# Source order for every engine beside the inverse, the scan and the output groups of a hybrid decoder layer, and two early x tiles

## Chip, cores and metric

The kernel runs on one core of one Trainium2 chip. The metric is the device time in microseconds of one execution, as the median of several runs. The profile is one further execution, taken by the hardware profiler.

## What is computed

One decoder layer on x of shape (1, 2048, 1024), float32:

```python
h = rms_norm(x, norm_w)
proj = h @ w_in                        # 1024 -> dn_qkv, dn_z, dn_b, dn_a, swa_q/k/v, swa_z, gates
o_dn = gated_delta_rule_chunked(...)   # 4 heads of 128, chunks of 64: a triangular solve per chunk,
                                       # then a scan over chunks with state S (128 x 128 per head)
o_dn = rms_norm(o_dn, dn_norm_w) * silu(dn_z)
for window, dilation in ((128, 1), (512, 4), (2048, 16)):
    ...                                # dilated sliding-window attention, o and its log denominator
o_swa = sum(softmax(lse over the three groups) * o) * silu(swa_z)
merged = sigmoid(g_dn) * (o_dn @ w_branch_dn) + sigmoid(g_swa) * (o_swa @ w_branch_swa)
out = x + merged @ w_out
```

## The kernel before

All large products are taken in two parts: each operand is split into a high part (ScalarE, `AF.Copy` into fp32r, L90) and the rest (VectorE or GpSimd, a subtraction, L91), and a product is three matmuls, high by high, high by low, low by high. The profile calls the engines PE (TensorE), ACT (ScalarE), DVE (VectorE), POOL (GpSimd) and SP (the queue from which the DMAs are issued).

TensorE's program is one long list. Everything else is hung on it by a clock of ticks: after every six of the large matmuls the kernel calls `hook()`, and `self.at(n, f)` calls f at the n-th hook from then. So the order of the source is a plan by hand: what stands at a tick is written into the program between the matmuls of that tick. Whether an engine's instructions run in that order is another question. Inside `tc.manual_schedule(engines=...)` the engines named keep the source's order; the others are ordered by a planner, by its own estimates of cost. `pinned(False)` names PE, ACT, DVE and POOL, `pinned(True)` SP as well. Each engine works its list off in order, each instruction waiting for what it needs.

The stages in the order of time:

- 0 to about 970 us: the projection for the attention (L436) with the attention beside it. Pinned; not touched.
- about 970 to 1990: `cunits`, 36 units of 128 columns of `w_in`. A unit has four blocks of 512 tokens, a block 24 matmuls of 512 columns (L723 to L725) into one of three "mm" PSUM tiles. Its weights come by DMA and are split in two halves, the next unit's at the fourth and the eighth hook after the first block of this one (`c_part`: ACT L90, POOL L91). Gate units (`g_block`) have ACT take tanh (L1161) out of PSUM into one of two "gt" tiles, which SP writes to DRAM (gscr, L1163); z units (`z_block`) do the same and add a VectorE operation (L1153) that reads PSUM once more.
- beside `cunits`, first the DeltaNet preparation (everything but SP pinned), and from `start_inverse` on, at about 1408 us, the following, with only PE pinned:
  - the inverse: VectorE reads Z (all 128 chunks' matrices, one per partition) and solves row by row, rows 1 to 63; a row is a product (L1023), two memsets and a sum (L1026), all on VectorE, and each row sets a tick for the next, more ticks the longer the row is. Row 64 copies (L1018) and writes the result to DRAM (vscr L1015, tscr L1019). The same ticks carry `combine(t)`, t = 0 to 15, ten ticks each, which merges the three attention groups: sums on VectorE (L1260, L1261), an exponential on ACT (L1262), shares and three weighings on VectorE (L1265 to L1271), two additions on POOL (L1276), and a write to osd by SP (L1278). `combine(0)` is called eight ticks after the inverse is set up.
  - the scan, at about 1768 to 1950: sixteen steps of three ticks, for two pairs of heads each. Stage 0: products with the state S into an "sc" tile (L1084, L1086), then rr on VectorE (L1088) and qs on ACT (L1091). Stage 1: a product (L1095), copied by ACT (L1097). Stage 2, for each pair: a product (L1101) into the single "po" tile, the state's update on VectorE (L1103), a product (L1106), its sum on VectorE (L1109), squares on ACT (L1113), a short chain on POOL (L1116 to L1120), and the scaling on VectorE (L1122), all of pair 0 and then all of pair 1 in the source. After both pairs `prep` for the next step: in stage 1 a product into an "sc" tile that VectorE reads (L1062, L1065), in stage 2 one that ACT reads (L1070, L1072). There are two "sc" tiles. The records of step t + 2 are loaded by SP at the end of step t.
  - from the last units on, the first weights of the next stage are loaded and split (`tail`, `w_split`).
- about 1990 to 2189: the fin phase, branch projections and gates, in eight blocks (`fin_y`), under `pinned(True)`. Products of weights for the output are formed beside it; two of them, T1 and T4, are parked in DRAM by way of the staging tiles "th" and "tl" of the pool `lp`, and fetched back in the last block.
- about 2189 to the end: eight output groups of 256 tokens (`group`), each seven Strassen-Winograd products of twelve matmuls (L1421 to L1423). The merged rows come back from DRAM as "mt" tiles (`m_load`, one group ahead), are summed and split four products ahead (`m_op`), the results are kept or added in "hold" tiles (ACT L1400, VectorE L1402, L1408), the residual x in "xo" tiles (loaded at the start of each group, four of 256 KB) is added, and SP writes the result. No engine is pinned here.

Of the kernel before, what the change touches and what calls it, by code (L numbers as in the profile page):

```python
# [6 lines left out]
F32 = mybir.dt.float32  # L7
F32R = mybir.dt.float32r
# [4 lines left out]
P = 128  # L13
T = 2048
D = 1024
# [28 lines left out]
def dr(ap, off, dims):  # L44
    return bass.AP(tensor=ap.tensor, offset=ap.offset + off, ap=[list(d) for d in dims])


class Net:
# [1316 lines left out]
    def m_op(self, q):  # L1365
# [8 lines left out]
        def new(n, a, b, how):  # L1374
            ss[n] = self.rawp.tile([P, 4, P], F32, name="raw")
            V.tensor_tensor(out=ss[n], in0=a, in1=b, op=how)  # L1376
# [8 lines left out]
        elif i == 4:  # L1385
            new("S4", part["A12"], ss["S2"], ALU.subtract)

    def group(self, g):
        nc, V, p2 = self.nc, self.nc.vector, self.p2
        acc, xo = {}, {}  # L1390
        hold = {"p1": p2.tile([P, 512], F32, name="hold", bufs=5)}

        def x_load(t, c):
            xo[t, c] = p2.tile([P, 512], F32, name="xo", bufs=4)
            nc.sync.dma_start(xo[t, c], dr(self.i["x"], (2 * g + t) * P * D + c * 512, [[D, P], [1, 512]]))

        def keep(n, pr, add=None):
            t = hold[n] = hold.get(n) or p2.tile([P, 512], F32, name="hold", bufs=5)
            if add is None:
                nc.scalar.activation(t, pr, AF.Copy)  # L1400
            else:
                V.tensor_tensor(out=t, in0=pr, in1=add, op=ALU.add)  # L1402

        def plus(n, t, c):
            nc.gpsimd.tensor_tensor(out=hold[n], in0=hold[n], in1=xo.pop((t, c)), op=ALU.add)

        def result(t, c, pr, add):
            V.tensor_tensor(out=add, in0=pr, in1=add, op=ALU.add)  # L1408
            nc.sync.dma_start(dr(self.out, (2 * g + t) * P * D + c * 512, [[D, P], [1, 512]]), add)
        for t, c in ((0, 0), (0, 1), (1, 1), (1, 0)):  # L1410
            x_load(t, c)
        if g == 0:
            self.m_load(1)
        for i, (_, tgt, first, wn) in enumerate(PROD):
            q = 7 * g + i
            self.at(1, lambda q=q: self.m_op(q + 4))
            if first:
                acc[tgt] = self.ps.tile([P, 512], F32, name="mm", bufs=3)
            pr = acc[tgt]
            ah, al = self.m_slot(q)  # L1420
            wh, wl = self.W[wn]  # L1421
            for k in range(4):
                mm = lambda x, y, **kw: nc.tensor.matmul(pr, x, y, **kw)  # L1423
                mm(ah[:, k, :], wh[:, k, :], start=first and k == 0, stop=False, skip_group_check=True)
                mm(ah[:, k, :], wl[:, k, :], start=False, stop=False, skip_group_check=True)
                mm(al[:, k, :], wh[:, k, :], start=False, stop=(k == 3), skip_group_check=True)
                if k % 2:
                    self.hook()
            if i == 0:
                keep("p1", pr)  # L1430
            elif i == 1:
                keep("u2", pr, hold["p1"])
                plus("u2", 0, 1)
            elif i == 2:
                result(0, 0, pr, xo.pop((0, 0)))
            elif i == 3:
                keep("u3", pr, hold["p1"])
                plus("u3", 1, 1)
                plus("p1", 1, 0)
            elif i == 4:  # L1440
                result(1, 1, pr, hold["u3"])
            elif i == 5:
                result(1, 0, pr, hold["p1"])
            else:
                result(0, 1, pr, hold["u2"])

    def run(self):
        from functools import partial
        tc = self.tc
# [3 lines left out]
        E = mybir.EngineType  # L1453
        pinned = lambda sync: tc.manual_schedule(engines={E.PE, E.Activation, E.DVE, E.Pool} | ({E.SP} if sync else set()))
# [53 lines left out]
        pin = ExitStack()  # L1508
# [9 lines left out]

        def start_inverse():
            self.nb_out()  # L1520
            pin.close()
            pin.enter_context(tc.manual_schedule(engines={E.PE}))
            dst.close()
            self.cb = pool(bst, "cb")
            self.inverse(pool(ist, "ip", "right"), start_scan)
# [31 lines left out]
        gu = [partial(self.g_block, j) for j in range(16)]  # L1557
        du = [partial(f, h) for h in range(H) for f in (self.k_block, self.q_block, self.v_block)]
        self.cunits(zu[:3] + du + gu[:12] + zu[3:] + gu[12:], {3: open_dn, 15: lambda: self.at(9, start_inverse)}, tail)
        self.flush()  # L1560
        pin.close()
# [7 lines left out]
        with pinned(True):  # L1569
            for nb in range(8):  # L1570
                if nb < 7:
                    self.o_plan(nb + 1, 4)
                if nb == 0:
                    for c in range(4):
                        self.at(1 + 28 * c, lambda c=c: self.wo_chunk(c))
                if nb == 7:
                    self.m_load(0)
                for m in range(8):
                    self.fin_y(nb, m)
                    if nb == 7 and m in (1, 3):  # L1580
                        self.fetch("T1" if m == 1 else "T4")
                    if nb == 7 and m < 4:
                        self.at(4, lambda m=m: self.m_op(m))
            self.flush()
        fst.close()
        self.p2 = pool(p2st, "p2", "right")
        for g in range(8):
            self.group(g)
        self.flush()
        p2st.close()  # L1590
        lst.close()
        ost.close()
# [40 lines left out]
```

## Time and profile before

| what | value |
|---|---|
| three runs | 2352.99 to 2355.91 us, median 2355.55 |
| profiled execution | 2355.83 us |
| its span, first to last instruction | 2353.8 us |
| instructions | 43662 |
| TensorE: busy, share | 2275.0 us, 97% |
| VectorE, ScalarE, GpSimd: busy | 1435.6, 919.8, 941.2 us |

The span is what the trace shows; the execution's own time is 2.0 us more. A view by stretches gives the busy time of each engine between two times; the waits give, for one engine and line, how long the engine stood idle ahead of that line's instructions and which instruction ended the idling; the timeline lists single instructions, with the idling ahead of one in brackets. In the timeline several instructions of a line can be joined (x4), and times of neighbours overlap, since an instruction is shown from its start to its last write.

### The profile page before, as it was taken

To read this page: it belongs to the slowest core of one execution; us is meant where nothing else is said; L and a number is where in the kernel's file an instruction comes from. 1 tells how busy PE (TensorE), PEld (TensorE's weight loads), DVE (VectorE), ACT (ScalarE), POOL (GpSimd) and SP (SyncE) were. 2 spreads that over 40 slices of the span, in tenths; PEclk is the share of its full clock that TensorE was granted. 3 is DMA by queue.
4 is the path that set the end of the run, shared out by engine and by line. 5 is a ranking of instruction groups with operands and counts; after the bars stand their busy time and mean duration, and the time that the engine had idled before them with its cause. 6 is when DMAs were issued, how large, how long until landed. Compare 5 with 4: busy or idle time off the path is not lost. (4 is left out here: it accounts for less than half of the span.)

```text
span 2353.8 us, 43662 instructions
## 1 busy us (share of the span) xinstructions
PE 2275.0 (97%) x15120; PEld 2063.3 (88%) x15120; DVE 1435.6 (61%) x2980; ACT 919.8 (39%) x2959; POOL 941.2 (40%) x1299
## 2 busy tenths in 40 slices
PE   7999999989999999999999999999999999999999
PEld 7999999889999999888788888777788888999787
DVE  6566586694445545446777768999813443666653
ACT  5345466653434435444666651111113333211221
POOL 6374265575303303303675563334212332332543
PEclk9999999999999999999999999999999999999999
DMA  9989889857887888853554445444345657787752
GB/s 304 325 279 322 276 276 292 271 160 247 259 258 239 250 272 262 257 145 98 127 131 123 117 108 181 144 127 134 126 143 164 196 170 229 232 277 240 249 157 89
DMA packets 557267, 485.80 MB, mean 206 GB/s; under 512 B 68280, under 2 KB 517112, under 8 KB 554104
## 3 DMA queue, kind: packets, MB, share of 16 engines
q1 hardware_dynamic: 556760, 482.95, 66.7%
q8 instruction: 120, 1.97, 0.3%
q14 instruction: 99, 0.81, 0.1%
q10 hardware_dynamic: 288, 0.07, 0.0%
HBM read 280.23 MB, written 202.67 MB: 205 GB/s over the span
## 5 line engine op out<-in xcount | busy, mean ns | idle before, releaser
L723 PE MATMUL mm<-hh,w 128*128 128x512 f32 x1152 | 465.2, 404 | 13.2 <-ACT gt L1161 9.8
L725 PE MATMUL mm<-hh,w 128*128 128x512 f32 x1152 | 458.2, 398 | 0.0
L724 PE MATMUL mm<-hl,w 128*128 128x512 f32 x1152 | 457.6, 397 | 0.0
L436 PE MATMUL mm<-w,hh 128*128 128x256 f32 x1760 | 326.8, 285 | 0.0
L723 PEld LDWEIGHTS mm<-hh,w 128*128 128x128 f32 x1152 | 220.8, 192 | 62.3 <-ACT gt L1161 12.9
L436 PEld LDWEIGHTS mm<-w,hh 128*128 128x128 f32 x1760 | 270.2, 189 | 0.0
L725 PEld LDWEIGHTS mm<-hh,w 128*128 128x128 f32 x1152 | 217.4, 189 | 46.9
L436 PE MATMUL mm<-hh 128*128 128x256 f32 x880 | 257.5, 293 | 0.0
L724 PEld LDWEIGHTS mm<-hl,w 128*128 128x128 f32 x1152 | 218.1, 189 | 41.9
L436 PE MATMUL mm<-hl,hh 128*128 128x256 f32 x880 | 249.7, 284 | 0.5 <-POOL hl L298 0.5
L436 PE MATMUL mm<-hh,hl 128*128 128x256 f32 x880 | 249.6, 284 | 0.0
L436 PE MATMUL mm<-w,hl 128*128 128x256 f32 x880 | 248.0, 282 | 0.0
L91 POOL TENSOR_TENSOR w<-raw,w 128x512 fp32r<-128x512 f32 x68 | 95.0, 1402 | 287.2 <-ACT w L90 281.8
L610 DVE CUSTOM_DVE_ANT_0 p<-sc,mask 128x128 f32<-128x128 f32 (+1 forms) x192 | 70.1, 365 | 214.6 <-PE sc L607 84.3
L436 PEld LDWEIGHTS mm<-hl,hh 128*128 128x128 f32 x880 | 169.1, 192 | 0.9 <-POOL hl L298 0.9
L436 PEld LDWEIGHTS mm<-hh 128*128 128x128 f32 x880 | 169.2, 192 | 0.0
L436 PEld LDWEIGHTS mm<-hh,hl 128*128 128x128 f32 x880 | 168.8, 192 | 0.0
L371 POOL TENSOR_SCALAR st<-st 128x4 f32<-128x4 f32 x96 | 21.4, 223 | 367.4 <-ACT junk L370 365.4
L436 PEld LDWEIGHTS mm<-w,hl 128*128 128x128 f32 x880 | 165.6, 188 | 0.0
L837 DVE SCALAR_TENSOR_TENSOR acc<-xr,cw,acc 128x512 f32<-128x512 f32 x144 | 121.2, 842 | 16.7 <-ACT acc L835 11.5
L594 ACT ACTIVATE kq<-tp 128x256 fp32r<-128x256 f32 x148 | 56.3, 381 | 179.7 <-PE tp L587 178.8
L1276 POOL TENSOR_TENSOR oc<-oc 128x512 f32<-128x512 f32 x32 | 62.2, 1943 | 131.3 <-DVE oc L1271 72.9
(351 smaller groups left out, 5798.8 us busy)
## 6 DMA issues: line engine op xcount, KB each, us to landing
wdr<-w SPq DMA_DIRECT2D x56, 512.0 KB, 4.8
w<-wdr SPq DMA_DIRECT2D x54, 512.0 KB, 4.8
qk<-qks SPq DMA_DIRECT2D x212, 128.0 KB, 4.0
qks<-rec SPq DMA_DIRECT2D x96, 256.0 KB, 3.1
raw<-in_w_in_dram SPq DMA_DIRECT2D x68, 256.0 KB, 3.2
gscr<-gt SPq DMA_DIRECT2D x64, 256.0 KB, 4.0
gt<-gscr SPq DMA_DIRECT2D x64, 256.0 KB, 4.6
wdr<-hh SPq DMA_DIRECT2D x28, 512.0 KB, 4.5
```

Source lines behind the costliest of these rows:

```text
L91: eng.tensor_tensor(out=l, in0=raw, in1=h.bitcast(F32), op=ALU.subtract)
L371: nc.gpsimd.tensor_scalar(out=st[:, 0:4], in0=st[:, 0:4], scalar1=1.0 / P, scalar2=EPS, op0=ALU.mult, op1=ALU.add)
L436: mm = lambda x, y, **kw: nc.tensor.matmul(o, x, y, skip_group_check=True, **kw)
L594: nc.scalar.activation(h, src, AF.Copy)
L610: nc.vector.tensor_tensor_reduce(out=p[:, lo:hi], in0=sc[:, lo:hi], in1=self.mask[:, slot * P + lo:slot * P + hi], scalar=3e38, scale=-SCA ...
L723: nc.tensor.matmul(pr, wh[:, k, :], a, start=(k == 0), stop=False)
L724: nc.tensor.matmul(pr, wh[:, k, :], b, start=False, stop=False)
L725: nc.tensor.matmul(pr, wl[:, k, :], a, start=False, stop=(k == KT - 1))
L837: nc.vector.scalar_tensor_tensor(out=acc, in0=xr[:, j:j + 512], scalar=w[:, j:j + 1], in1=acc, op0=ALU.mult, op1=ALU.add)
L1276: nc.gpsimd.tensor_tensor(out=o, in0=o, in1=oc[:, g, :, 0:P], op=ALU.add)
```

## The change

Three things are changed.

`start_inverse` no longer ends the pinning of ACT, VectorE and GpSimd. Until the end of `cunits`, beside the inverse, the combining, the scan and the first splits of the fin phase, they keep the source's order; SP stays with the planner.

The eight output groups run under `pinned(True)`: all five keep the source's order.

The two x tiles that group 0 needs first are loaded in the last block of the fin phase, into "th" and "tl", which by then hold nothing that is needed, and not in "xo" tiles at the start of group 0.

```diff
+    def x_first(self):
+        self.x0 = []
+        for c, n in enumerate(("th", "tl")):
+            x = self.lp.tile([P, 4, P], F32R, name=n, bufs=1).bitcast(F32).rearrange("p a c -> p (a c)")
+            self.nc.sync.dma_start(x, dr(self.i["x"], c * 512, [[D, P], [1, 512]]))
+            self.x0.append(x)
+
     def group(self, g):
...
         def x_load(t, c):
+            if g == 0 and t == 0:
+                xo[t, c] = self.x0[c]
+                return
             xo[t, c] = p2.tile([P, 512], F32, name="xo", bufs=4)
...
         def start_inverse():
             self.nb_out()
-            pin.close()
-            pin.enter_context(tc.manual_schedule(engines={E.PE}))
             dst.close()
...
                     if nb == 7 and m in (1, 3):
                         self.fetch("T1" if m == 1 else "T4")
+                    if nb == 7 and m == 5:
+                        self.x_first()
                     if nb == 7 and m < 4:
                         self.at(4, lambda m=m: self.m_op(m))
             self.flush()
         fst.close()
         self.p2 = pool(p2st, "p2", "right")
-        for g in range(8):
-            self.group(g)
-        self.flush()
+        with pinned(True):
+            for g in range(8):
+                self.group(g)
+            self.flush()
```

## Prediction

> **What bounds the kernel now.** I read the page first: the busy line, then the stretches by stage, then TensorE's waits in each stage.
>
> ```profile
> span 2353.8 us, 43662 instructions
> ...
> PE 2275.0 (97%) x15120; PEld 2063.3 (88%) x15120; DVE 1435.6 (61%) x2980; ACT 919.8 (39%) x2959; POOL 941.2 (40%) x1299
> ```
>
> TensorE (PE) is the bound: 97% busy, the next engine at 61%. A change of order can therefore give only what PE now idles or runs at a lowered clock, and it can take whatever new idling it causes. The stretches that the change touches (columns: us, busy us of PE, PEld, DVE, ACT, POOL, granted PE clock, DMA share, GB/s):
>
> ```profile
> 1408.00:1768.00 360.00, 346.75 (x1480) 280.92 (x1479) 279.18 (x420) 53.87 (x107) 109.35 (x70) 0.99 0.47 142
> 1768.00:1950.00 182.00, 175.97 (x1213) 152.58 (x1213) 73.74 (x244) 66.10 (x261) 56.14 (x167) 1.00 0.60 174
> 1950.00:2189.00 239.00, 235.00 (x1836) 226.84 (x1835) 142.89 (x210) 53.60 (x91) 73.90 (x52) 1.00 0.81 257
> 2189.00:2353.80 164.80, 156.42 (x673) 126.65 (x671) 78.68 (x99) 34.53 (x57) 69.93 (x52) 0.99 0.46 149
> ```
>
> These are the inverse, the scan, the fin phase and the output groups. PE idles 13.25, 6.0, 4.0 and 8.4 us in them. Three shorter stretches inside the inverse show the clock:
>
> ```profile
> 1500.00:1560.00 60.00, 56.28 (x237) 45.37 (x237) 55.83 (x79) 7.85 (x17) 20.20 (x10) 0.97 0.47 137
> 1560.00:1620.00 60.00, 54.16 (x231) 43.07 (x230) 59.30 (x68) 9.62 (x22) 24.56 (x14) 1.00 0.45 133
> 1680.00:1740.00 60.00, 56.53 (x234) 45.77 (x233) 24.91 (x20) 8.28 (x14) 6.84 (x11) 0.94 0.56 182
> ```
>
> DVE is nearly full until 1620 and mostly idle by 1700, although its rows belong to ticks spread over the whole stretch: the planner runs the inverse ahead of its place. What PE waited for, stage by stage (total us, times, longest; two lines of the inverse, one of the scan, two of the output groups):
>
> ```profile
> PE mm L723 <- ACT gt L1161: 9.8, 7, 2.9
> PE mm L723 <- DVE M L1025: 3.5, 1, 3.5
> ...
> PE po L1101 <- DVE S L1103: 5.6, 16, 0.4
> ...
> PE mm L1423 <- ACT hold L1400: 2.3, 1, 2.3
> PE mm L1423 <- DVE hold L1408: 1.9, 1, 1.9
> ```
>
> and what SP, which carries the gate tiles away, waited for in the inverse:
>
> ```profile
> SPq L1278 <- POOL oc L1276: 137.0, 16, 14.5
> ```
>
> An osd write sits up to 14.5 us in SP's queue, waiting for POOL's add; the gscr writes behind it do not go, the two gt buffers stay full, ACT's tanh (L1161) waits, and PE waits for PSUM.
>
> **The change, part by part.** The sum is made against the profiled execution, 2355.83 us (0.3 us above the median of 2355.55; its span is 2353.8).
>
> *Inverse, now in source order.* These rows place it:
>
> ```profile
> 1408.18 0.27 PE L995 MATMUL tp<-ident,nbr 128*64 128x128 f32 x1
> ...
> 1421.24 7.55 DVE L1008 TENSOR_TENSOR M<-Z,nb 128x4096 f32<-128x4096 f32 x1 [12.47 <-DMA Z<-lscr]
> ...
> 1433.68 0.18 DVE L1260 TENSOR_REDUCE cs<-oc 128x4 f32<-128x12 f32 x1 [0.46 <-DMA oc<-oscr]
> ...
> 1440.42 0.21 ACT L1262 ACTIVATE cs<-cs 128x12 f32<-128x12 f32 x1 [4.92 <-DVE cs L1261]
> ...
> 1415.96 1.29 POOL L91 TENSOR_TENSOR w<-raw,w 128x512 fp32r<-128x512 f32 x1 [7.29 <-ACT w L90]
> ...
> 1439.06 1.29 POOL L1276 TENSOR_TENSOR oc<-oc 128x512 f32<-128x512 f32 x1 [0.69 <-DVE oc L1271]
> ...
> 1440.20 0.39 PE L723 MATMUL mm<-hh,w 128*128 128x512 f32 x1
> ...
> 1442.97 0.39 PE L723 MATMUL mm<-hh,w 128*128 128x512 f32 x1
> ...
> 1446.67 0.45 DVE L1023 TENSOR_TENSOR Z<-M 128x289 f32<-128x289 f32 x1
> ...
> 1686.12 4.29 DVE L1023 TENSOR_TENSOR Z<-M 128x3969 f32<-128x3969 f32 x1
> ```
>
> The two L723 rows are twelve matmuls apart, the first of a unit and the first that reads the second half of its weights: 2.77 us, so 0.231 each, 1.385 per tick of six, 5.54 per block of 24.
> What goes: 13.25 us of idling (L1161's 9.8 and the 3.5 behind row 63) and the half-clock time, (1−0.97)·60 + (1−0.94)·60 = 5.4. Together 18.7.
> What comes: the first DVE operation waits for a DMA to 1421.24 either way. The call of combine(0) lies 8 ticks behind L995, near 1408.2+11.1 = 1419.3, but DVE reaches it at 1433.68, 14.4 late, and ACT and POOL now wait in their queues where they used to work past it. Queued behind are the weight splits of the unit that starts at 1440.20. In the source the first half is split 15 ticks behind L995 (near 1429), after combine(0)'s two adds; before, the planner took such splits some 13 us early (1415.96). So it starts after 1439.06+1.29 and ends near 1441.7–2.2: PE waits 1.5–2.0. The second half stands behind the exponential of combine(1), whose place is after row 18. Row 17 began at 1446.67 with combine(1)'s vector work, exponential at 1440.42, hoisted ahead of it; some 5 us of that now follow, so row 18 ends near 1444.4 and the split, a scalar half (0.6, estimated as half of the POOL row) and 1.29 on POOL, near 1446.5–7.2. It is needed at 1442.97+1.8: another 1.7–2.8. One window at half clock may follow; the cheaper of the two above was 1.8. Sum 5–7; I take 7 for queues that I cannot see.
> Later the lag drains: row 63 costs about 2·4.29 = 8.6 us and has 9 ticks, 12.5 us; L1161 and the adds then run at their ticks, so neither the long osd wait nor the row-63 wait returns (three mm buffers give 11.1 us, more than one row). Net −11.7, bounds −15 (two small waits) and +4 (the lag of 14.4 paid whole, 1.8 and as much again at low clock for several splits, against 18.7: 18.7 − 14.4 − 8).
>
> *Hand-over.* Row 64's writes now go at their tick:
>
> ```profile
> 1695.82 0.46 SPq L1015 DMA_DIRECT2D vscr<-M  x1
> ...
> 1712.83 1.32 SPq L1052 DMA_DIRECT2D vb<-vscr  x2
> ...
> 1766.18 0.68 PE L1062 MATMUL sc<-t,lo 64*64 64x64 f32 x8
> ```
>
> From write to the load of vb took 17.0+1.3 us; the scan's first matmul comes 20 ticks (27.7) after row 64. It fits with 9 us over. The scan's memsets on POOL, now in order, may hold one split: 0 to +2, taken +0.5. Today the load is some 50 us early (1712.83 against 1766.18); that cover goes.
>
> *Scan.* One step's rows, from L1103 of head pair 0 to the next step's first products:
>
> ```profile
> 1855.38 0.60 DVE L1103 SCALAR_TENSOR_TENSOR S<-S,eglb,po 128x128 f32<-128x128 f32 x2 [1.61 <-PE po L1101]
> ...
> 1856.40 0.31 ACT L1113 ACTIVATE os<-qs 128x128 f32<-128x128 f32 x1 [3.28 <-DVE qs L1109]
> ...
> 1856.85 0.61 DVE L1103 SCALAR_TENSOR_TENSOR S<-S,eglb,po 128x128 f32<-128x128 f32 x2 [0.53 <-PE po L1101]
> ...
> 1857.17 0.19 POOL L1117 TENSOR_TENSOR oss<-oss 128x2 f32<-128x2 f32 x1 [6.11 <-ACT os L1113]
> ...
> 1857.90 0.38 ACT L1072 ACTIVATE vb<-sc 64x256 f32<-64x256 f32 x1 [0.81 <-PE sc L1070]
> ...
> 1858.73 0.48 DVE L1122 TENSOR_SCALAR os<-qs,oss 128x128 f32<-128x128 f32 x2 [0.94 <-POOL oss L1120]
> ...
> 1860.18 0.61 PE L1084 MATMUL sc<-S,rec 128*128 128x128 f32 x4
> ...
> 1861.46 1.12 DVE L1088 SCALAR_TENSOR_TENSOR rr<-sc,ksn,rec 128x128 f32<-128x128 f32 x4
> ...
> 1862.46 0.38 PE L1095 MATMUL tp<-rr,vb 128*128 128x128 f32 x2
> ```
>
> In the source, pair 0 ends with L1122 (os), which waits for ACT's squares and POOL's chain; only then come pair 1's L1103 and L1109. The planner did pair 1 first (1856.85 lies ahead of 1858.73), and ACT took L1072 (1857.90) ahead of pair 1's squares, behind which it stands in the source. L1072 frees the PSUM slot "sc" into which pair 1's L1084 (1860.18) writes. In order: os of pair 0 still at 1858.73; pair 1's L1103 from 1859.12; from L1103 to the squares is 1856.40−1855.38 = 1.02, hence squares at 1860.14 (1.7 behind 1858.4 or so, where they ran), to POOL's start 1857.17−1856.40 = 0.77, so done by 1860.83; L1072, 0.38 with its release, to 1861.2. PE wanted 1860.18: +1.0 per step. The second limit is near it: rr stands behind pair 1's os, which starts 1858.73−1857.17 = 1.56 after POOL's 1860.9; so rr from about 1862.9 instead of 1861.46, its first two done near 1863.5, where PE wanted L1095 at 1862.46: also +1.0, of which the first wait has paid all but 0 to 0.2. PE is 97% busy here and has no slack to take it up. Fifteen hand-overs between sixteen steps by 1.07: **+16**, bounds +12 (some steps covered) and +18; below nothing only by the first rival.
> Whether such waits cost clock too: 1560 to 1620 PE idled 5.84 us in single waits under 2 us at a clock of 1.00, so no. [...]
>
> *Fin phase.* Its splits at the end of the units leave the planner: 0 to +2, taken +0.5. x_first adds two DMA issues to a stretch in which PE waits 4 us of 239: nothing, unless SP, in order, holds them back; they have until group 0's third product.
>
> *Output groups.* Gone: L1400's 2.3, L1408's 1.9, and the clock,(1−0.99)·164.8 = 1.6. The row before the stall:
>
> ```profile
> 2207.65 0.50 PE L1423 MATMUL mm<-hh 128*128 128x512 f32 x1 [1.91 <-DVE hold L1408]
> ```
>
> L1408 stood behind DVE work on mt tiles that had not landed; on SP the planner had put group 2's tiles and four x tiles before them, where in source order two x tiles go first. ACT's keep (L1400) can no longer be passed by later splits. What now waits in order: a product's result behind m_op's sums; the next use of that accumulator is two products off, 5.5 us, against three DVE sums of 0.7. I take −5.0, bounds −5.8 (all of it) and 0 (mt late again); above nothing is the tail of the range, not its centre.
>
> Sum: −11.7 + 0.5 + 16 + 0.5 − 5.0 = +0.3, on 2355.83 and on the median alike: **2355.8 us**, no change (a measurement of this kernel can tell about 0.2%, 4.7 us). Adding the likely errors (inverse ±5, scan ±3, output ±2) the forecast's own range is 2349 to 2363.
>
> **Rivals.** *A, faster: the scan's waits do not reach PE.* Both limits rest on the L1072 and L1122 rows being held by pair 0's chain. If the slot that pair 1's L1084 takes is not L1072's, and ACT and POOL, which no longer run other work between, close the pair chains about 1 us sooner, +16 shrinks to +2 and the sum to −14: 2342. For it: POOL idled 6.11 us ahead of 1857.17, so its queue is not full. Against it: the chain has no idle time of its own to give (squares follow L1109 at once), two sc buffers go round in the order z, vb, pair 0, pair 1, and there are two limits, not one.
> *B, slower: the start of the inverse.* If the splits behind combine's exponentials and adds come late not for one unit but for two or three, because the lag of 14.4 drains slowly, the gain of 18.7 is spent: DVE is behind by d when the next unit (22.2 us later) starts, and each unit whose split is more than its lead late pays about 4 and 1.8 of clock. Splits are made 8 and 4 ticks (11 and 5.5 us) before their unit; so it decides where the lag at the second unit is above 5.5 us. With two more units: −11.7+11.6 = 0, total +12: 2368. Against it: rows 1 to 18 cost under 1.3 us against a tick of 1.385, and combine about 5 us in ten ticks.
> [...]
> *D, nothing changes*, the planner's order being nearly the source's: excluded for the scan and for SP's 137 us, where orders differ; 2355.5.
>
> **How the numbers follow.** Forecast 0.63 (same 0.31, faster 0.14, slower 0.18: ±7 around +0.3 passes both bounds, and a wait in an in-order queue that I have missed costs more often than it gains), A 0.14 (faster), B 0.16 (slower), C 0.03 (slower), D 0.04 (same). Faster 0.28, same 0.35, slower 0.37. Range: down to A's centre and up to B's, 2342 to 2368; half of A, half of B and C are left out, some 0.18.
>
> **What would show it.** Right: L1161's waits under 1 us in all between 1450 and 1768 and no PEclk of 0.94; a few us of PE waits on POOL w L91 near 1440–1447; in the scan a new PE wait at L1084 (released by ACT vb L1072) or L1095 of about 1.0, fifteen times, stage about 16 us longer; output waits under 1.5. Wrong: no L1084 waits (A), waits on L91 at three units or more (B), PEclk under 0.97 in the scan (C).

## The result

The changed kernel is slower: 2369.85 us (2368.92 to 2371.27) against 2354.32 us for the kernel before, measured beside it; the ratio is 1.0066, with a 95% interval of 1.0049 to 1.0084. The forecast of no change was wrong, and the time lies just above its range.

Its profiled execution has a span of 2368.1 us. First the page, then the stretches cut at the same times as before (us, busy us of PE, PEld, DVE, ACT, POOL, granted PE clock, DMA share, GB/s):

```profile
span 2368.1 us, 43661 instructions
...
PE 2280.1 (96%) x15120; PEld 2065.1 (87%) x15120; DVE 1448.3 (61%) x2980; ACT 913.9 (39%) x2959; POOL 946.7 (40%) x1299
```

```profile
1408.00:1768.00 360.00, 349.90 (x1491) 282.72 (x1490) 298.25 (x420) 55.34 (x114) 122.09 (x71) 0.99 0.46 141
1768.00:1950.00 182.00, 162.56 (x1111) 138.68 (x1109) 65.88 (x223) 57.13 (x233) 46.28 (x145) 1.00 0.59 170
1950.00:2189.00 239.00, 232.74 (x1762) 221.40 (x1763) 135.98 (x212) 56.31 (x112) 77.40 (x70) 1.00 0.76 233
2189.00:2368.10 179.10, 174.95 (x848) 146.51 (x846) 86.93 (x120) 36.05 (x64) 71.68 (x56) 1.00 0.53 177
```

PE idles 10.1 us in the first stretch (13.25 before), 19.4 in the second (6.0), 6.3 in the third (4.0) and 4.2 in the last (8.4). But stages have slid against the clock on the wall, so fixed windows mix them. It is better to follow TensorE's list, which is the same in both kernels, and to take the starts of the same matmuls: the first of the inverse, the first of the scan, the last L1101 of the scan, and the first of the output groups (L1433 here was L1423).

```profile
1410.83 0.27 PE L995 MATMUL tp<-ident,nbr 128*64 128x128 f32 x1
...
1772.04 0.61 PE L1084 MATMUL sc<-S,rec 128*128 128x128 f32 x4
...
1962.51 0.68 PE L1101 MATMUL po<-vn,rec 128*128 128x128 f32 x4 [0.35 <-DVE S L1103]
...
2209.61 0.40 PE L1433 MATMUL mm<-hh,oh 128*128 128x512 f32 x1
```

In the kernel before the last three start at:

```profile
1771.86 0.61 PE L1084 MATMUL sc<-S,rec 128*128 128x128 f32 x4
...
1942.41 0.68 PE L1101 MATMUL po<-vn,rec 128*128 128x128 f32 x4 [0.34 <-DVE S L1103]
...
2188.91 0.39 PE L1423 MATMUL mm<-hh,oh 128*128 128x512 f32 x1
```

With the last matmul (2349.59 before, 2363.57 after) the differences of these starts give the account:

| stretch | before | after | difference | forecast |
|---|---|---|---|---|
| up to L995 (nothing changed there) | 1408.18 | 1410.83 | +2.65 | 0 |
| inverse and hand-over | 363.68 | 361.21 | −2.47 | −11.7 + 0.5 |
| scan | 170.55 | 190.47 | +19.92 | +16 |
| to the first output product | 246.50 | 247.10 | +0.60 | +0.5 |
| output products | 160.68 | 153.96 | −6.72 | −5.0 |
| last matmul to the end | 4.20 | 4.49 | +0.29 | 0 |

The sum is +14.3, the difference of the spans. The first line is not the change: over all the profiled executions of this study that stretch took 1404.6 to 1417.3 us with the same code. The measured median passes the upper end of the range, 2368, by 1.85 us, much less than that, so which side of the edge it fell on is partly chance; what has to be explained are the lines of the table, the inverse above all. Kernels are therefore compared below by the length of a stage, and whole times only beside each other.

PE's waits in the changed kernel, in the inverse and in the scan (total, times, longest):

```profile
PE mm L725 <- POOL w L91: 6.5, 4, 3.2
PE mm L723 <- ACT gt L1161: 1.9, 2, 1.5
PE mm L723 <- ACT w L90: 1.5, 1, 1.5
...
PE sc L1084 <- ACT vb L1072: 14.6, 15, 1.1
PE po L1101 <- DVE S L1103: 5.6, 16, 0.4
PE tp L1095 <- DVE rr L1088: 1.5, 3, 0.6
```

In the output groups this view has no line left. The 9.8 us on L1161 are down to 1.9 and the 3.5 us behind row 63 are gone, but waits on weight splits have come, and in the scan the predicted wait at L1084 stands fifteen times.

One step of the scan, to be laid beside the step shown in the prediction:

```profile
1852.04 0.61 DVE L1103 SCALAR_TENSOR_TENSOR S<-S,eglb,po 128x128 f32<-128x128 f32 x2 [1.61 <-PE po L1101]
...
1855.46 0.48 DVE L1122 TENSOR_SCALAR os<-qs,oss 128x128 f32<-128x128 f32 x2 [2.48 <-POOL oss L1120]
1855.86 0.60 DVE L1103 SCALAR_TENSOR_TENSOR S<-S,eglb,po 128x128 f32<-128x128 f32 x2
...
1857.56 0.36 ACT L1072 ACTIVATE vb<-sc 64x256 f32<-64x256 f32 x1
...
1856.40 0.61 PE L1086 MATMUL sc<-S,rec 128*128 128x128 f32 x4
1857.98 0.71 PE L1084 MATMUL sc<-S,rec 128*128 128x128 f32 x4 [0.96 <-ACT vb L1072]
1858.52 0.61 PE L1086 MATMUL sc<-S,rec 128*128 128x128 f32 x4
```

VectorE waits 2.48 us for POOL's chain, then scales pair 0, and only then updates pair 1's state; the copy that frees the slot ends at 1857.92, and L1084 starts at 1857.98.

### The profile page after: what moved, and what is told of

Same layout as the page of the kernel before. It is cut to its first block, busy times and chain, and to the rows that moved or that the text cites. A ratio compares the mean times of both kernels' runs of the same rounds, so it can differ in the third digit from the quotient of the medians.

```text
span 2368.1 us, 43661 instructions
## 1 busy us (share of the span) xinstructions
PE 2280.1 (96%) x15120; PEld 2065.1 (87%) x15120; DVE 1448.3 (61%) x2980; ACT 913.9 (39%) x2959; POOL 946.7 (40%) x1299
## 5 line engine op out<-in xcount | busy, mean ns | idle before, releaser
L1276 POOL TENSOR_TENSOR oc<-oc 128x512 f32<-128x512 f32 x32 | 76.5, 2391 | 113.1 <-DVE oc L1271 110.3
```

The lines of the kernel that those rows point to most:

```text
L1276: nc.gpsimd.tensor_tensor(out=o, in0=o, in1=oc[:, g, :, 0:P], op=ALU.add)
```

## The experiments

Theory T: the stages add up, and each has one cause. In the output groups it is SP's order and the early x tiles; in the scan the order within the step; in the inverse the combining, which holds ACT and POOL because VectorE is late. The rivals stand with each run.

**The output part alone, and without the early x tiles.** Both keep the planner in inverse and scan; the second also drops `x_first`.

```diff
         def start_inverse():
             self.nb_out()
+            pin.close()
+            pin.enter_context(tc.manual_schedule(engines={E.PE}))
             dst.close()
```

> The output part alone (output groups in source order, early x tiles), the planner back in the inverse and the scan as in the kernel before. Theory T: the three stages add up, and the output part is worth by itself the 6.7 us that TensorE gains there between the two traces; so 6 to 7 us under the kernel before, about 2348, with no wait of 1 us or more in the output groups and no half-clock window there. Rival: the gain in the output groups came from what the slower stages ahead of them left behind (transfers further along when they begin); then under 3 us, 2351 or more, and the wait on the hold tiles is back.

Measured 2352.83 us beside 2359.26 for the kernel before, ratio 0.9966 (0.9952 to 0.9981); the output products take 153.84 us, as in the changed kernel, and the inverse and scan 362.3 and 179.5 us by TensorE's starts, as before (363.7 and 179.4; the scan here and below up to a later matmul of the units, 199.3 in the changed kernel). The gain of 6.8 us is the output part's own.

> As the run before it, but without the early x tiles: all four x tiles of group 0 are loaded at its start, in order ahead of the mt tiles of group 1. Theory T: what helped is the order of SP (mt tiles no longer behind group 2's tiles), so at most 1 to 2 us are lost against the run with early x tiles, 2348 to 2350; the mt tiles land some 2.5 us later and one wait of about 1 us on a hold tile may show. Rival: the early x tiles are what removed the waits; then the time goes back to within 2 us of the kernel before.

Measured 2355.76 us, ratio 0.9982 (0.9968 to 0.9995); the output products take 155.97 us, 2.1 more than with the early tiles. The wait is not on a hold tile, as expected, but on ACT's split of the mt tile:

```profile
PE mm L1430 <- ACT hh L90: 1.9, 1, 1.9
```

So of 6.8 us some 4.7 come from source order. The other 2.1 go with the early x tiles: without them four x tiles stand ahead of the mt tiles in SP's list, in place of two. But that rests on one trace, and the same wait stands in two runs below that have the early tiles (1.0 us with a combine every 13 ticks, 2.9 with the adds on VectorE), so the 2.1 are not shown to be theirs.

**The planner back in the scan.** In the changed kernel, `start_scan` ends the pinning of all but PE.

```diff
         def start_scan():
             ist.close()
+            pin.close()
+            pin.enter_context(tc.manual_schedule(engines={E.PE}))
             self.scan(pool(qst, "qp", "right"), start_fin)
```

> The changed kernel, but with the planner taking over again where the scan begins (as in the kernel before); inverse and output in source order. Theory T: the 19.9 us that TensorE loses in the scan are the order within the steps and nothing else, so they go: 2370 - 20 = 2350, steps of 10.9 us, no wait at L1084. Rival: the scan is slow because the inverse and its last writes come late and its loads are near their limit; then 2365 or more, with waits on the loads.

Measured 2353.02 us, ratio 0.9963 (0.9947 to 0.9979); the scan 179.5 us against 199.3, no wait at L1084. The loss is the scan's order, not what the inverse hands over.

**Source order in the scan, but another order.** Everything stays pinned; the end of a step is written as the planner had it.

```diff
...
+            if st == 2:
+                stage(t, 0, 2, xs[t, 0])      # products, state, sum
+                stage(t, 0, 3, xs[t, 0])      # squares, POOL chain
+                stage(t, 1, 2, xs[t, 1])
+                prep(t + 1, 1)                # L1070, L1072
+                stage(t, 1, 3, xs[t, 1])
+                for g in (0, 1):
+                    stage(t, g, 4, xs[t, g])  # scaling, write
...
```

> The changed kernel, everything still in source order, but the last part of each scan step written in another order: pair 0 with its squares and POOL chain, then pair 1's products, state and sum, then the copy L1072, then pair 1's squares and chain, and both pairs' scaling (L1122) last. Theory T: the loss is the order alone; steps go back to 10.9 us, no wait at L1084 or L1095, 2370 - 20 = 2350, the same as with the planner in the scan. Rival: in-order queues cost by themselves (each engine waits at more places than these two), so at most half comes back, 2360 or more.

Measured 2350.78 us, ratio 0.9960 (0.9937 to 0.9982); the scan 178.3 us, one less than with the planner. PE's waits in it:

```profile
PE po L1101 <- DVE S L1103: 5.6, 16, 0.4
```

In-order queues cost nothing in the scan by themselves; the order written down did.

**One of the two limits taken away.** Only the copy L1072 moves ahead of pair 1's squares; pair 1's state update still stands behind pair 0's scaling.

```diff
...
+                stage(t, 0, 2, xs[t, 0])
+                stage(t, 0, 3, xs[t, 0])      # squares, chain, scaling
+                stage(t, 1, 2, xs[t, 1])
+                prep(t + 1, 1)
+                stage(t, 1, 3, xs[t, 1])
...
```

> The changed kernel with one thing moved in each scan step: the copy that frees the sc slot (L1072) stands ahead of pair 1's squares; pair 1's state update still stands behind pair 0's scaling. Two-limits theory (as in the prediction): the wait at L1084 goes, but rr (L1088) still stands behind pair 1's scaling, so a wait of about 1 us at L1095 takes its place; the scan stays at 196 to 200 us (199.3 in the changed kernel, 179.4 before). One-limit rival: the sc slot is all; scan 180 to 183 us.

One execution, 2382.23 us; the scan takes 203.8 us. The wait has moved:

```profile
PE tp L1095 <- DVE rr L1088: 15.9, 15, 1.8
```

Two limits at about the same height, as the prediction had it: taking away the first gains nothing. That it is 4.5 us worse fits the clock: behind the two longest of these waits, of 1.8 us each, the granted clock was 0.57 from 1881 to 1889 us and 0.79 from 1968 to 1976, (1 − 0.57)·8 + (1 − 0.79)·8 = 5.1 us, where the changed kernel's scan kept 1.00. Why those two waits were longer than the others, mostly 0.9 to 1.0, is open.

**The combining later and wider.** In the inverse of the changed kernel, this is what a late split looks like; the rows are of POOL, ACT, VectorE and PE:

```profile
1560.37 5.03 POOL L1276 TENSOR_TENSOR oc<-oc 128x512 f32<-128x512 f32 x2 [8.76 <-DVE oc L1271]
1565.36 1.26 POOL L91 TENSOR_TENSOR w<-raw,w 128x512 fp32r<-128x512 f32 x1
1568.00 1.28 POOL L91 TENSOR_TENSOR w<-raw,w 128x512 fp32r<-128x512 f32 x1 [1.38 <-ACT w L90]
...
1567.19 0.21 ACT L1262 ACTIVATE cs<-cs 128x12 f32<-128x12 f32 x1 [12.30 <-DVE cs L1261]
1567.31 0.61 ACT L90 ACTIVATE w<-raw 128x512 fp32r<-128x512 f32 x1
...
1554.93 2.26 DVE L1023 TENSOR_TENSOR Z<-M 128x2025 f32<-128x2025 f32 x1
1560.81 3.46 DVE L1023 TENSOR_TENSOR Z<-M 128x2116 f32<-128x2116 f32 x1
1566.97 0.18 DVE L1261 TENSOR_TENSOR cs<-cs,oc 128x12 f32<-128x12 f32 x1
...
1566.67 0.77 PE L725 MATMUL mm<-hh,w 128*128 128x512 f32 x1 [3.22 <-POOL w L91]
```

ACT has stood 12.3 us at an exponential, and POOL 8.8 us at an add, each waiting for VectorE; the splits behind them come late and PE waits. In the whole stage ACT stands at the exponentials for this long, first after, then before (it costs by what stands behind it in the queue, in the rows above 3.22 us of PE):

```profile
ACT cs L1262 <- DVE cs L1261: 159.6, 16, 15.6
```

```profile
ACT cs L1262 <- DVE cs L1261: 113.9, 15, 12.3
```

And VectorE does not catch up, since it has hardly any time left: 57.32 us busy of 60 around this place, in the second row. The granted clock of 0.97 there is one stretch of low clock, 1.8 us lost (0.72 from 1566 to 1572, and 0.50 from 1568 to 1570); the 0.94 at the start of the stage is two (0.66 from 1446 to 1451 and 0.57 from 1454 to 1458).

```profile
1410.00:1470.00 60.00, 55.20 (x224) 43.38 (x223) 41.55 (x137) 8.50 (x18) 12.55 (x10) 0.94 0.50 163
1540.00:1600.00 60.00, 56.78 (x239) 46.09 (x238) 57.32 (x66) 8.85 (x20) 26.16 (x13) 0.97 0.48 135
```

The repair to be tried gives it room (two changes at once, the start and the spacing):

```diff
-        self.at(8, lambda: self.combine(0))
+        self.at(36, lambda: self.combine(0))
...
-            self.at(10, lambda: self.combine(t + 1))
+            self.at(12, lambda: self.combine(t + 1))
```

> The changed kernel; the combining starts 36 ticks after the inverse is set up in place of 8, and a combine every 12 ticks in place of 10 (it still ends with the inverse). Load theory: in the changed kernel rows and combining fill VectorE's time, so it runs 7 to 12 us behind its ticks all along, and ACT (at the exponential) and POOL (at the adds) are held with it, which makes weight splits late. With a late start and more room the lag falls under 5 us, waits on the splits under 2 us in all, and the stretch from the start of the inverse to the first scan product (361.2 us in the changed kernel, 363.7 before) falls to 347 to 351; the whole to about 2358 on the chip of the first measurement. Rival: the splits are late for another reason (their own transfers, or POOL's speed); 357 or more.

The stretch from L995 to the first L1084 falls from 361.2 to 348.8 us; the kernel takes 2360.61 us, ratio 1.0000 (0.9988 to 1.0011) with the slow scan still in it. L1260 starts 5.5 us behind the matmul ahead of which it is written at the first combine and less than 3 from the fourth to the thirteenth, against 3.8 to 12.5 us in the changed kernel from the third on, mostly 7 to 11. The lag goes and the late splits with it, as the load theory says. Matmul by matmul, of the 12.4 us the start gives 8.8 and the later waits some 8, and 4.6 are lost again near 1719 and at the scan's first products. One long wait is left, 3.3 us on a split at 1719, and its rows show something else:

```profile
1711.79 1.68 POOL L1276 TENSOR_TENSOR oc<-oc 128x512 f32<-128x512 f32 x1 [10.36 <-DVE oc L1271]
1713.43 5.31 POOL L91 TENSOR_TENSOR w<-raw,w 128x512 fp32r<-128x512 f32 x1
...
1712.82 4.80 DVE L1023 TENSOR_TENSOR Z<-M 128x3969 f32<-128x3969 f32 x1
```

A split that takes 1.3 us elsewhere took 5.31; it ended 1.1 us after the row product beside it.

**Wider alone.** Start at 8 ticks as in the changed kernel, every 13 ticks.

```diff
-            self.at(10, lambda: self.combine(t + 1))
+            self.at(13, lambda: self.combine(t + 1))
```

> The changed kernel with a combine every 13 ticks in place of 10, but still starting at tick 8. Load theory: the stall at the start (8.8 us at the first two unit boundaries) stays, the later ones (5 us at 1567, 1.7 at 1659) go, as VectorE catches up; from the start of the inverse to the first scan product about 354 us. Start theory: the lag comes from the first 14 us alone and is only handed on; spacing changes little, 359 or more, with the lag at the exponentials still 7 us and more past 1500.

One execution, 2368.03 us; the stretch takes 361.4 us, the number of the start theory, but not by its mechanism: the lag at L1260 falls from 14.5 us to under 6 from the fourth combine on, and the waits around 1567 and 1659 are gone. In their place stand 4.5 us at 1720 (again a split of 5.31 us beside row 63's product) and 2.4 us at the scan's first use of zs (L1065):

```profile
PE mm L725 <- POOL w L91: 7.4, 3, 4.5
...
PE sc L1070 <- DVE zs L1065: 2.4, 1, 2.4
```

So spacing drains the lag, as the load theory says, and its number was wrong because the waits were exchanged for others.

**The adds on VectorE.** This prices what POOL's adds and VectorE's rows do to each other.

```diff
-            nc.gpsimd.tensor_tensor(out=o, in0=o, in1=oc[:, g, :, 0:P], op=ALU.add)
+            V.tensor_tensor(out=o, in0=o, in1=oc[:, g, :, 0:P], op=ALU.add)
```

> The changed kernel with the two additions of each combine on VectorE in place of POOL. If the additions on POOL slow VectorE's rows that run beside them (a row product of 1936 elements took 3.27 us beside one, the next, of 2025, 2.26 without), the products of the rows fall from 117.9 us in all to about 107, which nearly pays for 32 additions of 0.69 us: lag as before, POOL is not held any more, the stretch to the first scan product 355 to 361 us. Rival: the long row products have another cause; then VectorE has 22 us more to do in 240, its lag grows to 15 us and more, and the stretch takes 366 us or more.

One execution, 2388.91 us; the stretch takes 369.9 us. The groups of VectorE, first of the changed kernel and then of this one (busy us, mean ns):

```profile
L1023 DVE TENSOR_TENSOR Z<-M 128x1 f32<-128x1 f32 (+62 forms) x63 | 117.9, 1872 | 0.7
```

```profile
L1023 DVE TENSOR_TENSOR Z<-M 128x1 f32<-128x1 f32 (+62 forms) x63 | 103.0, 1634 | 0.4
...
L1276 DVE TENSOR_TENSOR oc<-oc 128x512 f32<-128x512 f32 x32 | 22.0, 687 | 0.4
```

Both halves are true: without the adds beside them the row products take 14.9 us less, and VectorE still has 22.0 − 14.9 = 7.1 us more to do, its lag grows to 15 us, and PE waits 10.2 us on ACT's splits. A stage that was full was made fuller.

**Both repairs, two other placements of the combining, and the late combining with the planner.**

> The two repairs together: the changed kernel with the scan step in the other order and the combining late (36 ticks) and every 12 ticks. If the parts add up: inverse 349, scan 178, output 154 us, span about 2337 (2358.1 of the late combining less 21), some 0.7% under the kernel before. Rival: the scan's shorter steps bring its loads or the fin phase's start into the way; 5 us or more of it is lost there.

Measured 2335.04 us (2331.78 to 2338.94) beside 2356.35, ratio 0.9909 (0.9895 to 0.9923): the fastest version here. Inverse 350.3, scan 178.2, output 153.84 us; the parts add up. PE's waits in inverse and scan:

```profile
PE po L1101 <- DVE S L1103: 5.6, 16, 0.4
PE mm L725 <- POOL w L91: 3.3, 1, 3.3
```

> As the run before it, but a combine every 11 ticks, so that the last one ends ten ticks before the last row. The stall of 3.3 us at 1719 came from a weight split on POOL that ran 5.31 us beside the product of row 63, behind an add of combine 14. Port theory (POOL's operation beside a long VectorE product ends only after it): with the last combines out of the longest rows the split is not late and the stretch of the inverse is 343 to 346 us, span about 2333. Rival: the split falls beside a row product anyway, and the tighter combines bring the lag back: 349 us or more.

2342.77 us, ratio 0.9942 (0.9931 to 0.9954); the stretch 358.8 us. The rival's number: the lag at the first five combines is 6.4 to 9.5 us (2.2 to 5.5 with 12 ticks). But most of the loss is elsewhere: the split near 1713 still kept PE waiting 2.6 us, and a wait of 3.8 us for L1065 came.

> Both repairs, a combine every 12 ticks, the first after 30 ticks in place of 36, so that all combines, and the add ahead of the late weight split, come six ticks earlier than where one stall of 3.3 us (and a half-clock window of 6.8) was left near 1711. Port theory: that split no longer meets the product of row 63, the stall goes, the stretch of the inverse is 345 to 347 us in place of 350.3, the span about 2 to 5 us under 2330 apart from what varies ahead of the inverse. Rival: at 30 ticks VectorE has not caught up (it was still 5.5 us behind at 36), and another split meets another row product: 352 or more.

2349.33 us, ratio 0.9956 (0.9942 to 0.9969); the stretch 359.1 us. The rival's number again, by other places:

```profile
1693.84 0.79 PE L723 MATMUL mm<-hh,w 128*128 128x512 f32 x1 [5.06 <-DVE gt L1166]
...
1768.32 0.68 PE L1070 MATMUL sc<-vb,zs 64*64 64x64 f32 x8 [3.50 <-DVE zs L1065]
```

The first is a z block's VectorE operation (L1153 in the changed kernel) that came late behind rows and weighings, the second stands behind an ACT operation that waited 10.71 us for a zscr write; in SP's list, which the planner still orders, that write comes behind the scan's loads. In these two runs, where combine, z block and hand-over meet costs some 9 us, and the value of 36 and 12 is one that was found, not derived.

> The kernel with only the output part (planner in inverse and scan), with the combining late (36 ticks) and every 11 ticks. Tells whether source order is needed for what the late combining gives. If the planner still works far ahead of the ticks, it fills the room, the osd writes block SP as before and the stretch of the inverse stays at 358 to 364 us; if the place of the combines in the source is what matters, it falls to 345 to 350 here too.

2365.89 us, ratio 1.0039 (1.0028 to 1.0051); the stretch 377.1 us, worse than either expectation. The wait on the gate tiles is larger than in the kernel before (9.8 us):

```profile
PE mm L723 <- ACT gt L1161: 21.4, 4, 12.0
```

```profile
SPq L1278 <- POOL oc L1276: 146.1, 16, 14.3
```

So with the planner the later combines harm (362.3 to 377.1). Its partner in source order, at the same 36 and 11 ticks, is 358.8 us, against 361.4 with the combines in their old place (the scan in the other order in both): a gain of 2.6, not the 12.4 of 36 and 12. The planner at 12 ticks was not run.

## Why the prediction was wrong

**Inverse: the failed step.** The prediction's sum was +0.3 us, the traces give +14.3: the inverse with its hand-over came 8.7 above its −11.2, the scan 3.9 above its +16, the output 1.7 below its −5.0, 2.65 lie ahead of the inverse, where nothing was changed, and 0.4 is left for the rest. In the inverse, what goes was right: 18.7 us, and the places where the changed kernel gains on the one before sum to 18.3. What comes was not: 7 was taken, 15.8 came. The start, the two halves of one unit's weights, cost 8.8 in place of 5 to 7, for the reasons given (first half behind the adds, second behind the exponential of combine 1); but that exponential, expected soon after 1444.4, came at 1451.07, which is 1448.4 without the 2.65, and two stretches of low clock followed in place of one. The rest, 5.1 us at 1567, 1.7 at 1659 and 0.3 between, fell to the sentence "Later the lag drains: row 63 costs about 2·4.29 = 8.6 us and has 9 ticks, 12.5 us". It weighed rows against their ticks and left out that the combines share VectorE with them, and that rows and POOL's adds stretch each other (14.9 us of row products, by the run with the adds on VectorE). Its own numbers, added up, leave no room: a row's 8.6 of 12.5 us is 69%, and the combine's "about 5 us in ten ticks" of 1.385 another 36%. The 1500 and 1560 rows of the prediction showed VectorE 93 to 99% busy, and they were read as the planner running ahead; the row at 1540 shows 96% in order, too. It was a nearly full engine, and it did not drain: after the first combines the lag at L1260 went from 14.7 us to 6.5, and then it stayed between 3.8 and 12.5. Spacing alone shows it: with a combine every 13 ticks, from the same start, the lag drains and the waits at 1567 and 1659 go. How much of the late combining's 12.4 us is the load and how much a fortunate place stays open, since three other placements gave 358.8 to 361.4 us.

**Scan: right mechanism, size 16 for 19.9.** Both limits were where the prediction put them; the other order and the copy alone show it. The wait came to 0.97 on average (14.6 in fifteen) against 1.0. But a wait is counted from the end that the view gives the matmul before, and the cost runs from start to start: L1086 to L1084 is 1857.98 − 1856.40 = 1.58 us, and in the kernel before it was 0.44 by these rows,

```profile
1859.74 0.61 PE L1086 MATMUL sc<-S,rec 128*128 128x128 f32 x4
1860.18 0.61 PE L1084 MATMUL sc<-S,rec 128*128 128x128 f32 x4
1860.63 0.61 PE L1086 MATMUL sc<-S,rec 128*128 128x128 f32 x4
```

so 1.14, and the next start is 0.54 off in place of 0.45: 1.23 per step, 18.5 in fifteen, and the rest at L1095.

**Output: right.** All of its waits went, −6.7, somewhat beyond the bound of −5.8: a third wait of 0.4 us (L1402) was not in the sum, and the rest may be the same counting. Source order gave the larger part; what the early x tiles gave, at most 2.1, is not settled.

**Hand-over and fin phase: right**, within half a microsecond each.

**Rivals.** B named the mechanism that decided (splits behind combine's exponentials and adds, at more than one unit) and the time, 2368, the time partly by luck (its scan was +16); it got 0.16. Its ground was half right: the lag at the combine ahead of the second unit was 6.5 us, above the 5.5 it asked for, but that unit did not wait. The sixth did, at 1567, and at the tenth, at 1659, PE waited for a tanh (L1161) that stood behind an exponential; both because the load kept the lag, not because the first one drained slowly. A is refuted by fifteen waits. C, the clock falling in the scan, stands in the chances with 0.03; no run shows a fall after each of fifteen such waits. What the changed kernel showed in its place: over the scan's 200 us, fifteen waits of about 0.97 and sixteen of about 0.35 left the clock at 1.00:

```profile
1771.00:1971.00 200.00, 178.37 (x1201) 152.20 (x1200) 72.58 (x244) 63.44 (x260) 53.07 (x165) 1.00 0.55 159
```

Some longer waits were followed by a lowered clock: with only the copy moved, the two of 1.8 us, by the 0.57 and 0.79 given above, and in the inverse of the changed kernel the one of 3.22 us that ended at 1566.67, by 0.50 from 1568 to 1570. A wait of 1.86 us that ended at 1593.73 in the kernel before was not: the clock stayed at 1.00 from 1560 to 1620.

## What to carry to other kernels

Before an engine is put in source order, its load in that stage is to be added up from everything that shares it, neighbours' slowdown included: here, at 57.32 us busy of 60, VectorE was late all along, and what waited on it in order (ACT's exponential 12.3 us, POOL's add 8.8) handed the lateness to work that had nothing to do with it, splits that kept PE 3.2 us. In source order a step must be written so that nothing waits in a queue ahead of what the next step needs; the same pinning with the scan's lines in another order made the scan 21 us shorter (178.3 against 199.3). And a wait should be priced from start to start, not by the idle time shown (1.14 us against 0.96 at L1084).

## What the runs showed of the hardware

VectorE's row products (L1023) and POOL's additions and splits took longer beside each other. In the late combining POOL's split, 1.3 us alone, took 5.31 beside a product of 4.80 and ended 1.1 after it; with a combine every 13 ticks a split again took 5.31, beside the product of the same row. In the changed kernel the product of 2116 elements, begun 0.44 us after an add, took 3.46 where one of 2025 with none beside it took 2.26, and of the two adds there the one from 1560.37 took 1.68 and the one from 1562.13, behind it, 3.27. In the inverse this made some 15 us of VectorE's 118 us of row products, by the one execution with the adds on VectorE (117.9 against 103.0). What the expectations call the port theory is these durations and no more; what lies behind them no run here shows.
